# Token-order GLU, a three-engine rope and new buffer homes in a hybrid decoder block

## The chip, the cores and the metric

The kernel runs on the eight cores of one Trainium2 chip, one launch, one sequence of 2,048 tokens to a core. The time of a run is the device time of the slowest core, in microseconds (us). Each kernel was run several times, in alternation with the kernel before on the same chip, and all comparisons use such runs.

There is a second, slower state, whatever the kernel: in some executions the cores of one die, or of both, run at a lower granted TensorE clock and the whole takes longer. Runs in that state are left out below; "fast" means the others. A ratio is always the mean time of one kernel's fast runs over the mean of the other's in the same rounds, with a 95% interval, so it is not quite the ratio of the medians that stand beside it.

Names: PE is the matmul engine (TensorE), DVE is VectorE, ACT is ScalarE, Pool is GpSimd, SP is SyncE, which here only issues transfers. SBUF is a core's working memory, PSUM the buffer that matmuls write to, HBM the large memory of the chip; "granted clock" is the share of the full TensorE clock that the profile shows as allowed. Pool issues transfers too, on the software DMA queue; SP uses the hardware queue.

## The reference, cut to what matters

```python
D_MODEL, SEQ, D_FF = 2048, 2048, 5632
# per layer
xn = rms_norm(x, g_pre_mix)
q, k, v, u = split(xn @ w_in)                    # 1024, 256, 256, 1024 columns
q, k = rotary(q), rotary(k)                      # "rope"
attn = sliding_window_attention(q, k, v, sinks)  # window 128, blocks of 128 tokens
y = s5_ssm(u, ...)                               # diagonal complex scan, 64 groups of 16 channels
z = gelu(y)
ssm = z * sigmoid(z @ w_glu + b_glu)             # the GLU, 1024 channels
mix = concat(rms_norm(attn), rms_norm(ssm)) @ w_o
h = x + rms_norm(mix, g_post_mix)
out = h + rms_norm(swiglu(rms_norm(h)), g_post_ffn)   # feed-forward, 5632 wide
```

The result must agree with this within a tolerance.

## The kernel before

Instructions are first recorded, then put in one fixed order for each engine by a list scheduler inside the kernel. It uses priorities, dependences, and its own time estimate for each instruction. The lower its number `prio`, the earlier an instruction is placed. The estimates put nothing on the chip, but they decide the order, and on the chip each engine follows that order strictly.

The parts that the argument touches (cuts are marked `# ...`):

```python
# the scheduler's estimates
if eng == "vector":
    # ...
    return 0.065 + big / 960.0 / sp
# transfers: one pipe for all of them
b = max(dma_free, s + op.dur); dma_free = b + op.nb; op.fin = dma_free + 1.9

# rope: both products on DVE, straight from PSUM; the sum on Pool; ONE pair rA, rB
def rope(bk, tt, nh):
    n = nh * 64
    V.tensor_tensor(out=rA[:, 0:n], in0=ps[:, bk, 0:n], in1=cap(cosT, ...), op=ALU.mult)
    for t_ in range(2):
        V.tensor_tensor(out=rv[:, :, t_, :], in0=pv[:, :, 1 - t_, :], in1=cap(snT, ...), op=ALU.mult)
# in proj_q: qb = qr[tt % 2]; G.tensor_tensor(out=qb, in0=rA, in1=rB, op=ALU.add)
#            P.dma(qT[...], qb, transpose=True)

# GLU: z comes back from HBM by token residue j (token = 8 c + j)
wglu = sb(WSO, [128, 8, 1024], BF16)         # over the LAST projection's weights
def glu():
    P.dma(wglu[:, :, :], w_glu..., q="gpsimd")
    for tb in range(4):                      # 4 quarters of 512 tokens
        zt = zring[tb % 2]
        # ... two loads of z, four GELU of 1024 elements on ACT, SBUF to SBUF
        for e8 in range(8):
            mv = M1[:, e8, :].rearrange("p (c j) -> p j c", j=8)[:, 2*tb:2*tb+2, :]   # stride 8
            # 8 matmuls of 512 columns -> ps[bk]; tanh on ACT -> sg
            V.scalar_tensor_tensor(out=mv, in0=sg, scalar=1.0, in1=zt[:, e8, :], op0=ALU.add, op1=ALU.mult)
            G.tensor_tensor(out=sq, in0=mv, in1=mv, op=ALU.mult)
            T.matmul(ps[:, 7, :], lhsT=onesb, rhs=sq, ...)      # sum of squares over channels
        rstd(rbc, ps[:, 7, :], 1)
        for e8 in range(8):                  # the normalising multiply, in place
            V.scalar_tensor_tensor(out=mv, in0=mv, scalar=g_ssm[e8], in1=rbc, op0=ALU.mult, op1=ALU.mult)

# W_o in four quarters, 4 MB read and 2 MB written each
def load_wo(k):
    P.dma(Wo[k][:, :, :], w_o_v[:, 4*k:4*k+4, :], q="gpsimd")

# the order of recording and the priorities
# ... proj_u, ssm_pair 0..15, proj_q(0), proj_q(1)
P.prio = 300.0; load_w(0, 1024); proj_q(2)          # k and v, the last projection
# ... ssm_pair 16..31 at 90 + 6 q
P.prio = 400.0
attention(0); attention(1); glu()
for k in (3, 0, 1, 2): load_wo(k)
# then W_o projection of tile tt with attention of tile tt + 2; then feed-forward
```

The first two W_o quarters lie where the normalised input xnT lies, so they can load as soon as the last projection has read it. M1 holds the GLU's result, 8 x 2,048 bf16 per partition.

## Time and profile before

Median 2,960.0 us of 4 runs (2,955.1 to 2,963.3). The profiled run took 2,957.3 us on its slowest core.

| milestone, us from the start | before |
|---|---|
| the last input projection ends | 502.3 |
| first GLU matmul | 523.3 |
| last normalising multiply | 769.2 |
| first feed-forward matmul | 1,050.6 |
| end | 2,957.3 |

Below, "the GLU" is the stretch from the first GLU matmul to the last normalising multiply, and "the W_o stage" the stretch from there to the first feed-forward matmul.

The page's slices cut the span into 40 equal parts of 74 us. Each digit is a busy share in tenths; PEclk is the granted clock in tenths of full speed.

```profile
PE   3798997533698989999999999999999999999995
...
DVE  5828773477777731101101100002110010100003
...
PEclk9797898766899999999999999999999999999997
DMA  9775455600488879556556576669975565565545
```

From the sixteenth slice on, PE is full and nothing is to be had. The hole is in slices 8 to 11 (517 to 813 us): PE at 5, 3, 3 and 6 tenths, the clock at 7, 6, 6 and 8, and DVE at 4 and then 7.

The windows view gives the same in microseconds, for the stretches gap before the GLU, GLU, and W_o projection with attention. Columns: window, length, busy us of PE, PEld (weight loads), DVE, ACT and Pool with their instructions, granted clock, DMA share, GB/s.

```profile
502.00:523.00 21.00, 2.47 (x14) 1.11 (x14) 5.58 (x10) 5.28 (x6) 6.30 (x9) 0.63 0.89 144
523.00:769.00 246.00, 101.84 (x429) 41.83 (x436) 174.94 (x112) 68.40 (x87) 88.73 (x58) 0.68 0.23 54
769.00:1051.00 282.00, 246.21 (x1451) 116.30 (x1479) 194.18 (x323) 161.52 (x332) 105.42 (x115) 0.92 0.82 183
```

In the GLU's 246 us DVE works 175 and PE 102, at a clock of 0.68. Which DVE instructions these are, the groups view of that window shows (line, engine, operation, output<-inputs, shapes, count | busy us, mean ns | idle before); t_44 is M1:

```profile
L411 DVE SCALAR_TENSOR_TENSOR t_44<-t_44,t_54,t_53 128x512 bf16<-128x512 bf16 x32 | 75.0, 2660 | 21.6 <-ACT t_53 L411 21.6
L411 DVE SCALAR_TENSOR_TENSOR t_44<-t_144,t_142 128x512 bf16<-128x512 f32 x8 | 22.0, 2750 | 6.0 <-ACT t_144 L411 6.0
...
```

A multiply of 512 elements takes 2.66 us, a product of the group shown 2.75 (2.5 to 2.75 over all four groups). The chain of waits (start, length, what) confirms that runs of them end the stage, and shows what comes before it:

```profile
502.75 20.06 DMA t_143<-w_glu
...
600.89 23.26 DVE t_44 L411 x10
...
750.52 18.66 DVE t_44 L411 x8
```

The DMA view of the stretch around 500 us lists the issues with the time to landing; t_154 and t_155 are W_o quarters:

```profile
t_143<-w_glu POOLq DMA_DIRECT2D x1, 2048.0 KB, 20.1
t_154<-w_o POOLq DMA_DIRECT2D x1, 2048.0 KB, 30.7
t_155<-w_o POOLq DMA_DIRECT2D x1, 2048.0 KB, 39.9
```

In the same stretch SP's timeline (start, length, what) shows two attention transposes that took 10 and 23 us merely to be issued; ordinarily one takes 1.2:

```profile
508.31 9.67 SPq L411 DMA_TRANSPOSE t_150<-t_148  x1
518.02 22.97 SPq L411 DMA_TRANSPOSE t_151<-t_149  x1
```

PE did not feel this: it had the DVE-bound GLU to wait for anyway.

### The profile page before, as it was taken

How to read it: one execution, taken by the hardware profiler on the slowest of the kernel's cores; microseconds unless marked ns; L12 is line 12 of the kernel's file. 1: busy time of each engine (PE TensorE's matmuls, PEld its weight loads, DVE VectorE, ACT ScalarE, POOL GpSimd, SP SyncE). 2: the span in 40 equal slices, each digit the busy share in tenths (PEclk: the TensorE clock that was granted, in tenths of full speed). 3: DMA queues.
4: the chain of work that ended last, by engine and by line, in shares of the span. 5: the costliest groups of instructions: out<-in, count | busy, mean ns of one | idle time of the engine just before them, and what ended most of it. 6: DMA issues, size and time to landing. Idle time of an engine off the chain costs nothing.

```text
span 2957.3 us, 31078 instructions; the slowest of 8 cores (2936.6 to 2957.3 us)
## 1 busy us (share of the span) xinstructions
PE 2605.0 (88%) x12527; PEld 1199.9 (41%) x12768; DVE 909.2 (31%) x1293; ACT 627.3 (21%) x1217; POOL 559.5 (19%) x510
## 2 busy tenths in 40 slices
PE   3798997533698989999999999999999999999995
PEld 2444443211344434444444444444444444444442
DVE  5828773477777731101101100002110010100003
ACT  4534322421355641000000000012000000000002
POOL 4621332244343410000000111100000000011102
PEclk9797898766899999999999999999999999999997
DMA  9775455600488879556556576669975565565545
GB/s 199 197 155 121 82 111 109 120 22 15 114 192 194 192 161 127 71 72 86 72 72 86 72 131 102 101 91 245 199 114 74 70 84 76 71 103 79 75 71 211
DMA packets 489133, 335.38 MB, mean 113 GB/s; under 512 B 173216, under 2 KB 458272, under 8 KB 480288
## 3 DMA queue, kind: packets, MB, share of 16 engines
q0 software_dynamic: 252032, 159.46, 40.3%
q1 hardware_dynamic: 236960, 173.91, 22.3%
q8 instruction: 104, 1.70, 0.2%
q14 instruction: 37, 0.30, 0.0%
HBM read 398.26 MB, written 56.62 MB: 154 GB/s over the span
## 4 chain that ended last, share of the span: by engine, by line
PE 79%; DVE 8%; DMA 6%; ACT 2%; issue 2%; POOL 1%; SPq 1%; ACTq 0%; DVEq 0%; POOLq 0%
PE ps L411 79%; DVE t_44 L411 4%; DMA t_168<-w_up 2%; SPq L411 1%; DMA t_158<-x 1%; DMA t_143<-w_glu 1%; POOL t_146 L411 1%; DVE t_75 L411 1%; DMA t_167<-w_gate 1%; DMA t_188<-hscr 1%; DMA t_46<-t_113 1%; DVE t_76 L411 1%; ACT t_148 L411 0%; POOL t_147 L411 0%; DVE t_158 L411 0%
## 5 line engine op out<-in xcount | busy, mean ns | idle before, releaser
L411 PE MATMUL ps<-t_163,t_168 128*128 128x512 bf16 x1380 | 313.3, 382 | 18.3 <-DMA t_168<-w_up 16.9
L411 PE MATMUL ps<-t_163,t_167 128*128 128x512 bf16 x1380 | 310.9, 380 | 8.8 <-DMA t_167<-w_gate 7.4
L411 PE MATMUL ps<-t_163,t_166 128*128 128x512 bf16 x1377 | 308.6, 379 | 3.7 <-ACT ps L411 2.0
L411 PE MATMUL ps<-t_163,t_169 128*128 128x512 bf16 x1381 | 309.3, 379 | 1.4
L411 PEld LDWEIGHTS ps<-t_163,t_168 128*128 128x128 bf16 x1408 | 138.7, 99 | 185.6 <-issue 22.7
L411 PEld LDWEIGHTS ps<-t_163,t_167 128*128 128x128 bf16 x1408 | 138.2, 98 | 174.6 <-issue 9.8
L411 PEld LDWEIGHTS ps<-t_163,t_166 128*128 128x128 bf16 x1408 | 137.4, 98 | 168.4 <-issue 2.5
L411 PEld LDWEIGHTS ps<-t_163,t_169 128*128 128x128 bf16 x1408 | 137.6, 98 | 166.3
L411 DVE TENSOR_TENSOR t_183<-t_179,ps 128x512 bf16<-128x512 f32 x44 | 30.3, 688 | 427.4 <-PE ps L411 424.4
L411 ACT ACTIVATE ps<-ps 128x512 f32<-128x512 f32 x64 | 37.2, 582 | 574.8 <-DVE t_185 L411 286.5
L411 DVE TENSOR_TENSOR t_183<-t_181,ps 128x512 bf16<-128x512 f32 x44 | 30.3, 688 | 398.7 <-PE ps L411 398.7
L411 PE MATMUL ps<-t_48,t_43 128*128 128x512 bf16 x499 | 116.4, 390 | 8.0 <-DVE t_112 L411 6.6
L411 ACT ACTIVATE t_179<-ps 128x512 f32<-128x512 f32 x44 | 26.3, 597 | 421.5 <-PE ps L411 404.3
L411 ACT ACTIVATE t_181<-ps 128x512 f32<-128x512 f32 x44 | 26.3, 597 | 409.3 <-PE ps L411 409.3
L411 DVE TENSOR_TENSOR t_185<-ps,t_178 128x512 f32<-128x512 f32 x32 | 22.1, 690 | 277.4 <-PE ps L411 277.3
L411 POOL DMA_DIRECT2D t_167<-w_gate x22 | 25.2, 1144 | 423.3 <-PE ps L411 423.3
L411 POOL DMA_DIRECT2D t_166<-w_gate x22 | 25.3, 1148 | 392.8 <-PE ps L411 392.8
L411 DVE TENSOR_TENSOR t_179<-ps,t_178 128x512 f32<-128x512 f32 x8 | 5.5, 692 | 262.9 <-PE ps L411 255.6
L411 PE MATMUL ps<-t_156,t_44 128*128 128x512 bf16 x242 | 66.2, 395 | 20.2 <-DVE t_152 L411 18.3
L411 DVE SCALAR_TENSOR_TENSOR t_44<-t_44,t_54,t_53 128x512 bf16<-128x512 bf16 x32 | 75.0, 2660 | 21.6 <-ACT t_53 L411 21.6
L411 PE MATMUL ps<-t_174,t_183 128*128 128x512 bf16 x346 | 79.6, 379 | 0.9 <-DMA t_174<-w_down 0.6
L411 PE MATMUL ps<-t_172,t_183 128*128 128x512 bf16 x348 | 79.8, 379 | 0.2
(333 smaller groups left out, 3742.8 us busy)
## 6 DMA issues: line engine op xcount, KB each, us to landing
t_166<-w_gate POOLq DMA_DIRECT2D x22, 1024.0 KB, 9.1
t_168<-w_up POOLq DMA_DIRECT2D x22, 1024.0 KB, 10.8
t_167<-w_gate POOLq DMA_DIRECT2D x22, 1024.0 KB, 9.3
t_169<-w_up POOLq DMA_DIRECT2D x22, 1024.0 KB, 10.8
t_158<-x SPq DMA_DIRECT2D x16, 1024.0 KB, 6.4
hscr<-t_158 SPq DMA_DIRECT2D x16, 1024.0 KB, 5.3
t_184<-hscr SPq DMA_DIRECT2D x8, 1024.0 KB, 14.1
t_184<-ffscr SPq DMA_DIRECT2D x8, 1024.0 KB, 15.0
```

The lines of the kernel that those rows point to most:

```text
L411: inst = getattr(eng, m)(*a, **kw)
```

## The change

Its intent: take the strided writes out of the GLU. Each block of 128 channels of z is read back as it lies, 64 identity matmuls bring it into PSUM, and one GELU per 1,024 elements writes it to SBUF in token order. The GLU's products and multiplies are then contiguous. Half of its squares move from Pool to ACT. The rope's PSUM read moves to ACT, one product stays on DVE, the other goes to Pool, with work buffers doubled. SSM's rounding step moves from DVE to Pool. The input tiles, the SSM preparation, w_glu, one W_o quarter and the GLU buffers get other homes; an SSM work buffer called CL is doubled, and the buffer of SSM's scan result goes from two to one. In attention, two normalising multiplies become one instruction. The scheduler gets new time estimates (DVE 0.085 us more per instruction, Pool more per element, two DMA pipes that slow each other) and may use a second activation table set.

The core of the diff (buffer naming, homes and table sets are cut):

```diff
-            return 0.065 + big / 960.0 / sp
+            return 0.15 + big / 960.0 / sp
 ...
-                b = max(dma_free, s + op.dur)
-                dma_free = b + op.nb
-                op.fin = dma_free + 1.9
+                if e == "sync":
+                    b = max(hw_free, s + op.dur)
+                    if sw_free > b:
+                        hw_free = b + 1.6 * op.nb
+                        sw_free += op.nb
 ...
         def rope(bk, tt, nh):
+            rr, rA, rB, _ = rbuf[tt % 2 + (2 if nh == 4 else 0)]
-            V.tensor_tensor(out=rA[:, 0:n], in0=ps[:, bk, 0:n], in1=cap(cosT, ...), op=ALU.mult)
+            A.activation(out=rr[:, 0:n], in_=ps[:, bk, 0:n], func=AF.Copy)
+            V.tensor_tensor(out=rA[:, 0:n], in0=rr[:, 0:n], in1=cap(cosT, ...), op=ALU.mult)
             for t_ in range(2):
-                V.tensor_tensor(out=rv[:, :, t_, :], in0=pv[:, :, 1 - t_, :], ...)
+                G.tensor_tensor(out=rv[:, :, t_, :], in0=pv[:, :, 1 - t_, :], ...)
 ...
-            V.tensor_scalar(out=k[:, :], in0=y[:, :], scalar1=MAGIC, scalar2=MAGIC, ...)   # SSM rounding
+            G.tensor_scalar(out=k[:, :], in0=y[:, :], scalar1=MAGIC, scalar2=MAGIC, ...)
 ...
-        wglu = sb(WSO, [128, 8, 1024], BF16)
+        wglu = sb("wglu", WSO + 16 * KB, [128, 8, 1024], BF16)
+        def zconv():
+            for b in range(8):
+                zr = zraw[b % 2]
+                P.dma(zr[:, :, :], zscr[:, b * 128:(b + 1) * 128, :].rearrange("j p c -> p j c"), ...)
+                for h in range(2):
+                    bk = 4 + 2 * h
+                    for k in range(4):
+                        T.matmul(ps[:, bk + k // 2, ...], lhsT=identb[:, :],
+                                 rhs=zr[:, 2 * k:2 * k + 2, h * 128:(h + 1) * 128], start=True, stop=True)
+                    A.activation(out=zT[h][:, b, :].rearrange("p (c j) -> p c j", j=8),
+                                 in_=ps[:, bk:bk + 2, :].rearrange("p a (j c) -> p c (a j)", c=128), func=AF.Gelu_apprx_tanh)
 ...
-                    mv = M1[:, e8, :].rearrange("p (c j) -> p j c", j=8)[:, 2 * tb:2 * tb + 2, :]
-                    V.scalar_tensor_tensor(out=mv, in0=sg..., scalar=1.0, in1=zt[:, e8, :]..., ...)
-                    G.tensor_tensor(out=sq..., in0=mv, in1=mv, op=ALU.mult)
+                    V.scalar_tensor_tensor(out=M1[:, e8, ts_], in0=sg[:, :], scalar=1.0, in1=zt[:, e8, zs], ...)
+                    if e8 % 2 == 0:
+                        G.tensor_tensor(out=sq[:, :], in0=M1[:, e8, ts_], in1=M1[:, e8, ts_], op=ALU.mult)
+                    else:
+                        A.activation(out=sq[:, :], in_=M1[:, e8, ts_], func=AF.Square)
 ...
-        Wo = [sb(o_, ...) for o_ in (0, 16 * KB, WSO + 16 * KB, SO + 16 * KB)]
+        Wo = [sb("Wo", o_, ...) for o_ in (0, 16 * KB, WSO, SO + 16 * KB)]
 ...
         P.prio = 400.0
+        zconv()
         attention(0)
         attention(1)
         glu()
```

With w_glu moved, three W_o quarters, and no longer two, become loadable when the last projection ends: the third lies over that projection's weights.

## The prediction

> **What bounds it now.** The page's 40 slices show PE 95% busy from about 1,100 us to the end (feed-forward blocks, not changed). The loss lies before. Busy time by stretch: in 600 to 800 us PE is 45% busy, DVE 77%, granted clock about 0.7; in 150 to 475 us PE is 93% busy; in 820 to 1,050 us (W_o projection with attention) about 90%.
>
> The timeline dates the GLU: first matmul at 523 us, last normalising multiply at 769 us, so 246 us. PE's work there is 288 matmuls of 512 columns, at the 0.219 us of the feed-forward stage 63 us. The limit is DVE: 32 products of 2.5 to 2.75 us and 32 multiplies of 2.66 us (groups, 161 us together), because M1 is written with stride 8 elements. Four runs of multiplies stand in the chain of waits with 84 us. The Trainium skill, "SBUF — State Buffer", section "Door 1: The DMA port swizzle", says SBUF has 16-byte lines and that going to a new line each time pays a penalty; stride 8 bf16 is 16 bytes. The trace agrees: a contiguous 128x2048 instruction of this kind takes 2.37 us, about 0.6 us per 512 elements. Before the GLU, PE waits 14 us for w_glu, issued at 502.8 us because it lies in the last projection's weight buffer.
>
> **The change, costed.**
> - z to token order: 64 short identity matmuls (about 8 us PE); GELU keeps 16 instructions of 1,024 elements (1.05 us now; from PSUM with stride I assume 1.1 to 1.5), partly behind the k/v projection: 5 to 10 us exposed.
> - GLU: DVE 64 x about 0.65 = 42 us instead of 161; half the squares go to ACT. PE-bound: 9 x 0.219 = 2.0 us per step, 16 per quarter, plus 1 to 2 us for table loads (1.28 us each): 70 to 80 us. Saves about 165 us.
> - w_glu in the other weight buffer, free earlier: saves 14 to 20 us.
> - W_o: three quarters load after the k/v projection (43 us for three loads in the trace), one after half the GLU (it lies under z): ready about when the GLU ends.
> - Rope: DVE 1.5 us per tile falls to 0.7; ACT +0.6, Pool +1.5. PSUM frees sooner, so PE in 250 to 325 us (20 of 25 us busy, clock 0.65) fills better. SSM buffers no longer lie under preparation buffers, and the doubled CL removes Pool's 48 us of waiting on its store, so SSM may start before 209 us. Saves 20 to 35 us.
> - W_o stage: PE-bound, about 17.5 us per tile (DVE 14.5): same length, about 293 us after the GLU.
>
> **Sum.** 165 + 17 + 27 - 10 = about 200 us, nearly all on the critical path. Predicted 2,760 us, 2,715 to 2,815. Faster by over 2%: 0.96; within 2%: 0.03; slower: 0.01.
>
> **What would show it.** GLU 70 to 90 us; M1 writes 0.6 to 0.7 us; granted clock there above 0.9 (the skill, "TensorE: Matmul & The Clock Gate", Part 1: an idle PE falls to half clock, consistent with 0.7 here); no wait for w_glu; first feed-forward matmul near 850 instead of 1,050 us; feed-forward unchanged, about 1,860 us after the last W_o matmul.
>
> **What would make it wrong.** Pool and DVE slowing each other in the rope (a square on Pool took 9.5 us beside DVE's strided multiplies, 1.1 alone); GELU's PSUM read at stride 512 bytes costing 2 us or more; the last W_o quarter landing late; identity matmuls in PE's fixed order waiting for z loads.

## The result and the profile after

The changed kernel takes 2,878.95 us, the median of 4 runs (2,862.1 to 2,889.1); before 2,960.0. The ratio of the fast runs is 0.9722, interval 0.9668 to 0.9775: faster, by 82 us by the medians, where 200 were forecast. The result is correct. Within the fast runs there is a small spread: in two of the four, die 0 had a granted clock of 0.948 and took 2,884 to 2,887 us, against 0.958 and 2,858 to 2,862 us on die 1. The profiled run is one without that, 2,860.5 us, so the traces differ by 97 us. On undisturbed dies alone, the slowest cores of the changed kernel have a median of 2,860 us here and of 2,865 in its repeat below, which is about 0.967 of the kernel before.

| milestone, us | before | after | forecast (worked out from the sums of the prediction) |
|---|---|---|---|
| the last input projection ends | 502.3 | 486.7 | 475 |
| first GLU matmul | 523.3 | 551.7 | 489 |
| last normalising multiply | 769.2 | 659.6 | 570 |
| first feed-forward matmul | 1,050.6 | 941.6 | 851 |
| end | 2,957.3 | 2,860.5 | 2,758 |

The forecast column subtracts 27 (rope and SSM) from the first row; starts the GLU after a gap of 21 - 17 + 10 = 14 us; gives the GLU 246 - 165 = 81 us; and leaves the rest as it was. Against it, the profiled run loses 12 us in the projections, 51 us in the gap, 27 us in the GLU, 1 us in the W_o stage and 12 us in the feed-forward part.

The slices of the page after, to be held against those before:

```profile
PE   3789998489888989999999999989999999999994
...
DVE  7635863176766310001110000012111000000003
...
PEclk9789998689998989999999999999999999999997
DMA  9685743637888875646566666589965564665545
```

The hole has shrunk from four slices to one, the eighth (501 to 572 us): PE at 4 tenths, DVE at 1, and the clock at 6. The windows of the same three stretches:

```profile
487.00:552.00 65.00, 15.82 (x75) 8.19 (x73) 2.06 (x4) 21.31 (x23) 5.10 (x8) 0.54 0.83 160
552.00:660.00 108.00, 92.51 (x464) 39.95 (x462) 75.03 (x112) 70.96 (x104) 40.16 (x43) 0.90 0.37 81
660.00:942.00 282.00, 243.81 (x1463) 115.29 (x1464) 194.29 (x298) 158.04 (x324) 119.07 (x117) 0.93 0.83 181
```

The GLU shrank from 246 to 108 us and PE is now its busiest engine. The W_o stage is unchanged at 282. But the gap before the GLU grew from 21 to 65 us, in which PE works 16 and the DMA engines are 83% busy. The M1 writes did what was asked of them; the first line is the normalising multiply, the second one of four groups of products:

```profile
L430 DVE SCALAR_TENSOR_TENSOR M1.2_44<-M1.2_44,sm.12_54,rbc.11_53 128x512 bf16<-128x512 bf16 x32 | 26.3, 890 | 2.8 <-ACT rbc.11_53 L430 2.8
...
L430 DVE SCALAR_TENSOR_TENSOR M1.2_44<-sgb.115_157,zT.112_154 128x512 bf16<-128x512 f32 x8 | 7.7, 958 | 3.9 <-ACT sgb.115_157 L430 3.9
...
```

What PE waits for between 480 and 662 us (waited for: us in total, times, longest):

```profile
PE ps L430 <- DMA zraw.109_151<-zscr: 27.7, 2, 27.0
PE ps L430 <- DMA zraw.110_152<-zscr: 17.4, 3, 14.0
PE ps L430 <- ACT sgb.114_156 L430: 5.3, 3, 2.4
```

Waits for two of the eight z loads cost 27 and 14 us, 41 together. Later ones are quick, as the chain of waits shows:

```profile
491.51 42.52 DMA zraw.110_152<-zscr
...
538.44 4.18 DMA zraw.109_151<-zscr
...
```

And this is their company; the DMA view of 480 to 560 us, size and time to landing:

```profile
Wo.124_166<-w_o POOLq DMA_DIRECT2D x1, 2048.0 KB, 17.8
Wo.125_167<-w_o POOLq DMA_DIRECT2D x1, 2048.0 KB, 29.2
Wo.126_168<-w_o POOLq DMA_DIRECT2D x1, 2048.0 KB, 42.5
zraw.109_151<-zscr SPq DMA_DIRECT2D x3, 512.0 KB, 15.2
zraw.110_152<-zscr SPq DMA_DIRECT2D x3, 512.0 KB, 3.8
```

Pool issues three W_o quarters between 487 and 490 us, in the same moment in which SP issues the first z loads:

```profile
487.62 0.38 SPq L430 DMA_DIRECT2D zraw.109_151<-zscr  x1
...
491.51 7.76 SPq L430 DMA_DIRECT2D zraw.110_152<-zscr  x1
520.32 7.25 SPq L430 DMA_DIRECT2D zraw.109_151<-zscr  x1
536.16 0.36 SPq L430 DMA_DIRECT2D zraw.110_152<-zscr  x1
```

The first of these lands at 518 us, the second at 534, with the last W_o quarter, and the third, issued at 520, at 535. The three issued after that take about 4 us each, as did the two before the burst. Not one of the conversion's matmuls ran under the k and v projection: the first stands at 486.6 us, and the projection ended at 486.7. It is the burst that had held up two attention transposes before the change, when it cost nothing.

### The profile page after: what moved, and what is told of

Read it like the earlier page. It is cut to its first block, busy times and chain, and to the rows that moved or that the text cites. A ratio compares the mean times of both kernels' runs of the same rounds, so it can differ in the third digit from the quotient of the medians.

```text
span 2860.5 us, 31526 instructions; the slowest of 8 cores (2832.4 to 2860.5 us)
## 1 busy us (share of the span) xinstructions
PE 2606.5 (91%) x12832; PEld 1199.6 (42%) x12832; DVE 792.9 (28%) x1133; ACT 662.9 (23%) x1286; POOL 631.1 (22%) x622
## 4 chain that ended last, share of the span: by engine, by line
PE 80%; DMA 7%; DVE 4%; issue 3%; ACT 2%; POOL 1%; SPq 1%; ACTq 0%; DVEq 0%; POOLq 0%
PE ps L430 80%; DMA wup.138_180<-w_up 2%; DMA zraw.110_152<-zscr 1%; SPq L430 1%; DMA wgt.137_179<-w_gate 1%; DMA PT.120_162<-Pb.118_160 1%; DMA hring.158_200<-hscr 1%; DVE xs.34_76 L430 1%; DVE M1.2_44 L430 1%; ACT L427 0%; DMA idf.27_69<-ident 0%; ACT Pb.118_160 L430 0%; DVE TT.63_105 L430 0%; DVE xs.33_75 L430 0%; DVE ast.23_65 L430 0%
## 5 line engine op out<-in xcount | busy, mean ns | idle before, releaser
L430 PE MATMUL ps<-hnT.133_175,wgt.137_179 128*128 128x512 bf16 x1408 | 313.0, 381 | 15.8 <-DMA wgt.137_179<-w_gate 15.8
L430 PE MATMUL ps<-hnT.133_175,wup.138_180 128*128 128x512 bf16 x1408 | 312.3, 380 | 8.3 <-DMA wup.138_180<-w_up 8.3
L430 PE MATMUL ps<-hnT.133_175,wgt.136_178 128*128 128x512 bf16 x1408 | 311.1, 379 | 2.4 <-DMA wgt.136_178<-w_gate 2.4
L430 PE MATMUL ps<-hnT.133_175,wup.139_181 128*128 128x512 bf16 x1408 | 310.9, 379 | 0.0
L430 PEld LDWEIGHTS ps<-hnT.133_175,wgt.137_179 128*128 128x128 bf16 x1408 | 138.0, 98 | 183.9 <-issue 19.3
L430 PEld LDWEIGHTS ps<-hnT.133_175,wup.138_180 128*128 128x128 bf16 x1408 | 138.0, 98 | 175.9 <-issue 11.1
L430 PEld LDWEIGHTS ps<-hnT.133_175,wgt.136_178 128*128 128x128 bf16 x1408 | 137.9, 98 | 168.6 <-issue 2.9
L430 PEld LDWEIGHTS ps<-hnT.133_175,wup.139_181 128*128 128x128 bf16 x1408 | 137.7, 98 | 166.2
L430 DVE TENSOR_TENSOR hid.153_195<-ev.149_191,ps 128x512 bf16<-128x512 f32 x44 | 30.2, 687 | 438.2 <-PE ps L430 435.4
L430 DVE TENSOR_TENSOR hid.153_195<-ev.151_193,ps 128x512 bf16<-128x512 f32 x44 | 30.2, 687 | 390.5 <-PE ps L430 390.5
L430 ACT ACTIVATE ev.149_191<-ps 128x512 f32<-128x512 f32 x44 | 26.3, 597 | 420.5 <-PE ps L430 406.5
L430 ACT ACTIVATE ev.151_193<-ps 128x512 f32<-128x512 f32 x44 | 26.3, 597 | 399.0 <-PE ps L430 397.5
L430 PE MATMUL ps<-ws.6_48,xnT.1_43 128*128 128x512 bf16 x512 | 117.5, 386 | 0.0
L430 POOL DMA_DIRECT2D wgt.137_179<-w_gate x22 | 25.1, 1141 | 413.1 <-PE ps L430 413.1
L430 POOL DMA_DIRECT2D wgt.136_178<-w_gate x22 | 25.3, 1148 | 393.4 <-PE ps L430 393.4
L430 PE MATMUL ps<-Wo.124_166,qT.3_45 128*128 128x512 bf16 x256 | 71.6, 405 | 21.4 <-DVE Ab.129_171 L430 18.6
L430 PE MATMUL ps<-wdn.144_186,hid.153_195 128*128 128x512 bf16 x352 | 80.0, 379 | 0.8 <-DMA wdn.144_186<-w_down 0.8
L430 PE MATMUL ps<-wdn.147_189,hid.153_195 128*128 128x512 bf16 x352 | 80.1, 379 | 0.0
L430 PE MATMUL ps<-wdn.140_182,hid.153_195 128*128 128x512 bf16 x352 | 80.1, 379 | 0.0
L430 PE MATMUL ps<-wdn.146_188,hid.153_195 128*128 128x512 bf16 x352 | 80.1, 379 | 0.0
```

Of the source, the lines that this page charges most:

```text
L430: inst = getattr(eng, m)(*a, **kw)
```

## The experiments

The first theory: the burst of W_o loads beside the z loads makes the stall, and the stall is most of the miss. The rivals: the time merely moves to another wait; or the miss lies in the GLU and W_o stage themselves. There were eighteen runs, one of them the changed kernel again, in six batches, each batch beside the kernel before on its own chip. Every edit also lets the scheduler reorder the instructions around it. Gains over the changed kernel are given from both its ratios, 0.9688 and 0.9722; the second contains the two runs in which die 0 had less clock. On undisturbed dies alone (median of their slowest cores) the ratio is about 0.967 for the changed kernel and 0.956, 0.958, 0.947, 0.955 and 0.936 for experiments 1, 11, 12, 13 and 15, so the lower end of each range is the safer one.

### 1. The z conversion earlier

```diff
+        P.prio = 290.0
         zconv()
+        P.prio = 400.0
```

The z of a block is complete well before the last projection ends; with a priority ahead of the k and v projection its loads come before the burst.

> The changed kernel with the z conversion given a better priority than the k/v projection, so that its matmuls stand among the projection's and its z loads are issued before the three W_o loads. Theory (z loads caught behind W_o loads): the first GLU matmul moves from 551.7 to about 490-500 us after the start, the loads of z land in 3 to 6 us each, W_o still arrives in time, the total falls by 45 to 60 us, to about 2,825 us (ratio to before about 0.955). Rival (the conversion is slow by itself: 512-byte pieces, two buffers, PE taken from the projection): the conversion takes as long, the projection ends later by about as much, and the total falls by less than 15 us.

Measured: 2,839 us, ratio 0.9569 [0.9548, 0.959]. The conversion lies at 449 to 484 us, wholly under the projection, and the first GLU matmul comes at 488. So the 65 us gap is gone, but only 35 to 45 us of it are gained (0.0119 to 0.0153 of 2,960, against the changed kernel's 0.9688 to 0.9722). The chain of waits shows who now stands beside the burst:

```profile
493.54 37.51 DMA PT.120_162<-Pb.118_160
```

An attention transpose takes 37.5 us, and PE waits 20 us for that buffer. The stall was real, but the GLU now takes 152 us in place of 108, so a good part of its worth turned into other waits.

### 2. The W_o loads held until z has landed

```diff
-            P.dma(Wo[k][:, :, :], w_o_v[...], q="gpsimd")
+            P.dma(Wo[k][:, :, :], w_o_v[...], q="gpsimd", rk=[("zl", b) for b in range(8)])
```

> The changed kernel with the W_o loads made to wait until the last z load has landed; nothing else moves. Theory (contention with W_o): after the k/v projection the remaining z loads take about 4 us each, the conversion ends near 510-515 us, the GLU starts there instead of at 551.7 us, and W_o, landing by about 560-570 us and its last quarter by about 590 us, is still ahead of the W_o projection: total 30 to 45 us less, about 2,840 us. Rival (the conversion is slow by itself): the GLU starts at 540 us or later and the total is the same or longer, because W_o now comes later.

Measured: 2,862 us, ratio 0.9646 [0.9617, 0.9675]. The z loads beside the conversion take 4.6 to 5.7 us each and the conversion 26 us in place of 61, which shows that the burst made them slow. The first GLU matmul comes at 526 us. But PE then waits 18.9 us for one attention transpose, and the first feed-forward matmul comes at 940.5 us, as with the stall.

### 3. The old kernel with contiguous writes alone

Wrong result: the kernel before, M1 written in phase order (relative error 0.71).

```diff
-  mv = M1[:, e8, :].rearrange("p (c j) -> p j c", j=8)[:, 2 * tb:2 * tb + 2, :]
+  mv = M1[:, e8, tb * 512:(tb + 1) * 512].rearrange("p (a c) -> p a c", a=2)
```

> The kernel before with the two GLU writes of M1 made contiguous (phase order, so the result is wrong on purpose); no conversion, no moved buffer, same rope. Theory (stride of 16 bytes is the cost of the GLU): the 128x512 writes fall from about 2.7 to about 0.7 us, the GLU from 246 to about 95-105 us, the total by 130 to 150 us, to about 2,820 us, which is below the changed kernel. Rival (the GLU is bound by something else, such as PE's clock or ACT's table loads): the writes get faster but the total falls by less than 80 us.

Measured: 2,900 us, ratio 0.9765 [0.9746, 0.9785], a gain of 70 us and not 130 to 150. The products fall to 0.80 us and the multiplies to 1.25; the GLU falls from 246 to 148 us, so 98 us are won there. The GLU starts 4 us later, and the W_o stage grows from 281 to 305 and gives back a quarter. The stride is the cause of the slow GLU, and what a stage wins is not what the kernel wins.

### 4. The old rope

```diff
-            A.activation(out=rr[:, 0:n], in_=ps[:, bk, 0:n], func=AF.Copy)
-            V.tensor_tensor(out=rA..., in0=rr[:, 0:n], ...)
+            V.tensor_tensor(out=rA..., in0=ps[:, bk, 0:n], ...)
             for t_ in range(2):
-                G.tensor_tensor(out=rv..., ...)
+                V.tensor_tensor(out=rv..., ...)
```

> The changed kernel with the rope back on DVE from PSUM (its buffers kept). If the rope split is what moved the end of the projections from 502 to 487 us, that end goes back to 500 us or later and the total rises by 10 to 25 us, to about 2,895 us. Rival (the gain before the GLU comes from the buffers' new homes, or Pool and DVE hinder each other so that the split is worth nothing): the end of the projections stays within 5 us of 487 us and the total within 8 us.

Measured: 2,908 us, ratio 0.9816 [0.9787, 0.9845]; the projections end at 527 us, 41 us later than in the changed kernel, and even 25 us later than in the kernel before, which has the same rope on DVE. Read alone, this says that the rope move is worth 30 us or more. It is read again under 14.

### 5. to 8. Four parts that might matter

Number 6 spreads W_o in 16 pieces over the GLU steps, on top of experiment 1:

```diff
-            P.dma(Wo[k][:, :, :], w_o_v[:, 4 * k:4 * k + 4, :], q="gpsimd")
+            at = {0: (0, 1, 3, 4), 1: (6, 7, 9, 10), 2: (12, 13, 15, 16), 3: (18, 20, 22, 24)}[k]
+            for c in range(4):
+                P.dma(Wo[k][:, c, :], w_o_v[:, 4 * k + c, :], q="gpsimd", rk=[("g", at[c])])
```

> The conversion early as in the first experiment, and W_o loaded in 16 pieces of a quarter of its 4 loads, each tied to a step of the GLU, so that the software queue never holds 12 MB at once. In the first experiment the conversion was hidden, but a transpose of attention issued at 493.5 us took 37.5 us to land, beside three W_o loads issued at 488 to 491 us, and the GLU lasted from 488 to 625 us. Theory (any load on the other queue waits out a burst of W_o): transposes land in 3 to 6 us throughout, the GLU ends at 580 to 595 us, total about 30 to 40 us below the first experiment: about 2,800 us (ratio 0.944 to 0.948). Rival (the transposes and the GLU are slow for another reason, for example PE's clock after the projections, or W_o simply needs that bandwidth): the GLU still ends after 610 us and the total is within 12 us of the first experiment, or W_o arrives late and PE waits for it by as much.

Missed. Only two of its runs were fast, 2,877 us, ratio 0.9696 [0.9663, 0.9729], and the profile fell in the slow state (read on a core of the undisturbed die). The pieces were issued in bunches, at 495 to 501, 516 to 524 and 545 to 562 us, and PE waited 31 us in three waits for attention transposes behind them. A wait tied to steps of work does not spread transfers when the work itself runs in spurts.

Number 7 has all squares on Pool, as before the change (`if e8 % 2` and the ACT branch taken out):

> The changed kernel with all squares of the GLU on Pool again instead of half on ACT. In the contiguous variant of the kernel before, the normalising multiplies took 1.25 us beside Pool's squares, 0.89 us in the changed kernel. Theory (DVE with two inputs in SBUF and Pool reading SBUF take turns): the multiplies' mean goes from 0.89 to about 1.2 us, the GLU (first matmul to last multiply, 108 us) gets 10 to 20 us longer, total 8 to 20 us more. Rival (ACT, with twelve table loads, is the GLU's limit): taking the squares off ACT shortens the GLU, total lower by 5 us or more.

Measured: ratio 0.9654 [0.9583, 0.9725], lowest 2,851 us. The multiplies rise from 0.89 to 1.11 us and the GLU from 108 to 118, as expected, but the W_o stage gives the 10 us back: the first feed-forward matmul comes at 943.6 us. The share of ACT in the squares bought nothing in the total. The means hide two cases: in the changed kernel 25 of the 32 multiplies took 0.74 to 0.75 us, and the 7 that lay for over 0.5 us beside a square on Pool took 1.1 to 1.6; in this run 15 took 0.74 to 0.76 us and 17 took 1.1 to 1.5, all beside squares or softmax masks on Pool.

Number 5 restores the old homes of the input tiles and the SSM preparation:

> The changed kernel with x, its gain and the normalised rows back under the query buffer, and the preparation buffers back under the SSM buffers (doubled CL kept). Theory of the prediction (the new homes let the SSM start earlier): the second u projection ends at 236 us or later, the first SSM matmul comes later than 200 us by 5 us or more, the total rises by 5 to 15 us. Rival from the trace (new homes only let SSM loads of weights into the SP queue early, where they hold up the preparation's small transfers; PE waits 12.5 us for Kst): the second u projection ends at 224 us as before the change, and the total is the same or up to 12 us less.

Measured: 2,867 us, ratio 0.9665 [0.9639, 0.9692]; SSM's first matmul at 209.8 in place of 200.6 us, the projections end at 485.9. The homes make SSM start 9 us earlier and are worth nothing at the end.

Number 8 is the changed kernel once more:

> The changed kernel itself once more, on the same chip as the other three, as the base for their differences. All theories: ratio to before 0.967 to 0.978 as on record; z loads that are issued after 487 us land in 27 to 43 us, the first GLU matmul at 545 to 560 us.

Measured: lowest 2,864.8 us, ratio 0.9688 [0.9627, 0.975]; the conversion at 482.3 to 544.5, first feed-forward matmul at 940.3 us. The stall repeats: 65.8 us from the projections' end to the first GLU matmul, against 65.0.

### 9. GLU before attention

On top of experiment 1, the GLU is recorded and ranked before the first two attention tiles, so that PE does not stand behind a late transpose.

```diff
         P.exp0 = True
+        glu()
+        P.prio = 405.0
         attention(0)
         attention(1)
-        glu()
+        P.prio = 400.0
```

> The conversion early as in the first experiment, and the GLU ahead of the first two attention tiles (recorded first, better priority), so that no instruction of PE in the GLU waits for a transpose while W_o is loading; W_o itself as in the changed kernel. Theory (a transfer on the critical path that shares the time of the W_o burst waits it out; none is left now): no wait of PE for PT above 3 us before the last GLU product, GLU from 488 to 570-580 us, first feed-forward matmul at 880 to 895 us instead of 918, total about 2,800 us, ratio 0.943 to 0.950. Rival (the time only moves: the attention tiles put off leave the W_o stage that much longer, because that stage is not limited by PE): the GLU ends early as above, but the feed-forward starts at 910 us or later and the ratio is 0.953 to 0.960, as in the first experiment.

Measured: ratio 0.9672 [0.9644, 0.97], lowest 2,854 us. The GLU ran at 497 to 604 us without a long wait, and the W_o stage, from the last multiply to the first feed-forward matmul, took 342 us in place of 282: attention must be done some time, and there it is in the way. The rival was right in kind; the ratio is worse than even it expected.

### 10. SSM's rounding back on DVE

```diff
-            G.tensor_scalar(out=k[:, :], in0=y[:, :], scalar1=MAGIC, ...)
+            V.tensor_scalar(out=k[:, :], in0=y[:, :], scalar1=MAGIC, ...)
```

> The changed kernel with the rounding step of the SSM tables back on DVE (32 instructions of 128x256). With the rope back on DVE the projections ended at 527 us, 25 us later than before the change, so something else of the change must cost time in that stretch. Theory (Pool is too loaded: tables on Pool come late for DVE): projections end at 475 us or earlier, total 5 to 15 us less. Rival (it is not this step): projections end within 5 us of 482 to 487 us, or later, total within 6 us or longer.

Measured: ratio 0.9689 [0.9661, 0.9718], the projections end at 487.7 us. The step is worth nothing here.

### 11. The old time estimates

The scheduler's estimates of the kernel before in the changed kernel (the first hunks of the diff undone). No instruction changes, only the order.

> The changed kernel with the time estimates by which it orders its instructions (cost of each instruction, two DMA queues) put back to those of before; the instructions are the same. Theory (the order is worth little): projections end and GLU start within 10 us of 482-487 and 548-552 us, total within 10 us. Rival (the new order is what costs or wins in the projections and in the W_o stage): projections' end or the time from last GLU product to the feed-forward's start moves by over 15 us.

Measured: 2,841 us, ratio 0.9595 [0.9576, 0.9614], against 0.9688 to 0.9722 of the changed kernel: 27 to 38 us (21 between the two profiled runs, neither of them disturbed). The z stall is all there (PE waits 28.5 and 15.3 us for z), the GLU starts at 552 us, and still the first feed-forward matmul comes at 924.5 us, 16 us earlier. PE's wait for DVE's output tile in the W_o stage falls from 18.6 to 2.3 us. The new estimates were made with care and gave a worse order.

### 12. Both helpers together

Experiments 1 and 11 in one kernel.

> The changed kernel with both edits that helped alone: the z conversion placed ahead of the k and v projection (which measured a ratio of 0.957 to the kernel before) and the scheduler's time estimates of the kernel before (0.960; the changed kernel alone 0.969 to 0.972). Theory: they act on different stretches, so their gains add. With the old estimates the z conversion is hidden in the k/v projection as well: first GLU matmul at about 488 us instead of 552, and the W_o stage after it keeps the short waits of DVE's output (about 2 us in place of 18 us), so the first feed-forward matmul comes at about 895 to 908 us, the time is 2800 to 2825 us and the ratio about 0.945 to 0.952. Rival: what the one gains the stage after it takes back, because the attention transposes wait behind the three W_o loads wherever the z loads do not, and because the order of the later stages comes out differently anyway: the first feed-forward matmul stays at about 915 to 925 us and the ratio at 0.955 or above.

Measured: 2,808 us, ratio 0.948 [0.946, 0.9499], correct, as the theory had it: the gains add. It beats both kernels. First GLU matmul 486, last multiply 627, first feed-forward matmul 893 us. The burst still shows, in SP's timeline:

```profile
491.73 8.39 SPq L417 DMA_TRANSPOSE PT.120_162<-Pb.118_160  x1
500.17 28.89 SPq L417 DMA_TRANSPOSE PT.121_163<-Pb.119_161  x1
540.14 1.96 SPq L417 DMA_TRANSPOSE PT.120_162<-Pb.118_160  x1
```

No attention transpose is issued between 500 and 540 us; attention's first tiles fall behind the GLU.

### 13. and 15. Without the burst

Moving the loads or the conversion only turned one wait into another, so no run had shown the time without the burst. Here the three early W_o quarters load a sixteenth of their columns, and the matmuls repeat it (wrong result, relative error 0.93; the same number of matmuls). Once in the changed kernel, once in the kernel of experiment 12.

```diff
+            n = 2048 if k == 3 else 128
-            P.dma(Wo[k][:, :, :], w_o_v[:, 4 * k:4 * k + 4, :], q="gpsimd")
+            P.dma(Wo[k][:, :, 0:n], w_o_v[:, 4 * k:4 * k + 4, 0:n], q="gpsimd")
 ...
+            if c < 12:      # 128 columns, read four times
+                rhs = cap(Wo[c // 4], (c % 4) * 2048, [[8192, 128], [0, 4], [1, 128]])
```

Two of the three small loads then go out well before the projections end (at 424.9 and 426.5 us in experiment 13), so they are not only smaller.

> The changed kernel with the three early W_o loads cut to a sixteenth each (128 of 2048 columns, repeated by the matmuls; wrong result on purpose, same number of matmuls). It shows what the burst of loads costs in all. Theory: the burst is the main part of the miss. The z conversion then runs at the pace of its own loads, about 25 us as in the run where W_o waited for z, the attention transposes land in under 6 us, the first GLU matmul comes at about 512 us, the first feed-forward matmul at about 895 to 910, and the ratio is 0.950 to 0.957 (the changed kernel alone 0.969 to 0.972). Rival: the time only moves into the in-order waits of the W_o stage, as it did in three runs before: the first feed-forward matmul stays at 925 us or later and the ratio at 0.962 or above.

Measured: 2,828 us, ratio 0.9554 [0.9533, 0.9576]. The conversion takes 25 us; the GLU starts at 524 us (the projections ended at 496 in this order), and the first feed-forward matmul comes at 912. The ratio is in the theory's range; that last mark is 2 us outside it. In the changed kernel the burst costs 40 to 50 us, all told (36 on undisturbed dies). And even without it the gap before the GLU is 28 us where the forecast had 14.

> The best version so far (z conversion ahead of the k/v projection, old estimates; measured ratio 0.948) with the three early W_o loads cut to a sixteenth (wrong result on purpose). Theory: what the burst still costs there is the waits for attention transposes, 16 us in PE's list of waits, and the order of work behind them; without the burst the first feed-forward matmul comes at about 865 to 880 us instead of 893, the time is 2775 to 2795 us and the ratio 0.937 to 0.943. Rival: these waits are off the limiting path, the W_o stage has its own limit, and the ratio stays at 0.945 to 0.950.

Measured: 2,768 to 2,789 us, ratio 0.9361 [0.9334, 0.9388]; the first feed-forward matmul at 849.6 us, where the prediction had it "near 850". By the ratios that is 35 us better than experiment 12, a little more than the theory expected. (The profiled run is the slowest of the four, 2,789 us, only 16 us better than that of experiment 12.) SP's timeline, in which the same transposes now go out one after another:

```profile
489.33 1.23 SPq L417 DMA_TRANSPOSE PT.120_162<-Pb.118_160  x1
492.69 1.23 SPq L417 DMA_TRANSPOSE PT.121_163<-Pb.119_161  x1
495.74 1.23 SPq L417 DMA_TRANSPOSE PT.120_162<-Pb.118_160  x1
```

In this kernel the GLU stage takes 106 us and the W_o stage 259, against 140 and 267 in experiment 12. PE's waits for transposes there came to only 16 us, so the list of waits understated the burst by half; the rest may be the order of work behind it, which was not tested.

### 14., 16. and 17. What the rope is worth

Experiment 4 had left a contradiction: the old rope made the changed kernel slower than its like in the kernel before. The first run here is experiment 4 with the old estimates.

> The changed kernel with the old rope (on DVE from PSUM) and the old time estimates in the scheduler. Theory: the old rope ended the projections at 527 us and not at 502 because the new estimates (DVE 0.09 us more per instruction) put the instructions in an order that suits the new rope alone: with the old estimates they end at about 500 to 508 us, the z stall stays at about 64 us, the first feed-forward matmul comes at about 945 to 955, ratio 0.967 to 0.973. Rival: the estimates are not the reason (the single R buffer, the z store's home, or the z conversion's effect on the order are): they end at 518 us or later, ratio about 0.977 to 0.982.

Measured: 2,833 us, ratio 0.9571 [0.9549, 0.9592], and the projections end at 477.7 us, earlier than either theory had it. This is no slower than the new rope with the same estimates (experiment 11: 0.9595 [0.9576, 0.9614], 486.6 us). So with these estimates the rope's move to three engines brings nothing; what experiment 4 measured was the new estimates, which suit the old rope badly (0.9816 against 0.9571). And with the old rope the projections now end 25 us earlier than in the kernel before. Of the differences left, two were tried: the rounding step and the doubled work buffers. Back to DVE with the rounding, on top of 14:

> e14 (old rope on DVE, old estimates) with SSM's rounding step back on DVE as well, as in the kernel before. Theory: what shortens the stretch is relief of DVE, and with the rope on DVE the rounding step, 32 instructions, is the relief that e14 still has; without it the stall of the kernel before comes back: granted clock about 0.7 in 250 to 325 us, the projections end at 492 to 505 us, ratio 0.962 to 0.969 (e14 0.957). Rival: the step is worth nothing here either: 476 to 484 us and 0.955 to 0.959.

Measured: 2,835 us, ratio 0.9548 [0.9499, 0.9597], the projections end at 481.0 us. Not the rounding. Single work buffers, on top of 14:

```diff
-            rr, rA, rB, _ = rbuf[tt % 2 + (2 if nh == 4 else 0)]
+            rr, rA, rB, _ = rbuf[2 if nh == 4 else 0]
```

> e14 (old rope on DVE, old estimates) with single work buffers for the rope's two products, as in the kernel before. Theory of the buffers: with one pair, DVE must wait for Pool's sum of the last tile before it writes the next, so PSUM is held longer; the projections end at 490 to 505 us and the ratio is 0.962 to 0.969. Rival: DVE is busy with other work meanwhile, 476 to 484 us and 0.955 to 0.959.

Measured: 2,862 us, ratio 0.9639 [0.9592, 0.9686], and the projections end at 496.2 us, 18.5 later. So single buffers cost most of the 25 us, a gain that the prediction had put down to the rope's move. DVE's waits up to the projections' end show one way. First the kernel before, 225 to 502 us, where t_111 is the rope's first product and t_113 Pool's sum, which must have read the product of the tile before; then experiment 14; then experiment 17:

```profile
DVE t_111 L411 <- POOL t_113 L411: 25.9, 7, 15.1
```

```profile
DVE rA.73_115 L417 <- POOL qr.75_117 L417: 2.7, 1, 2.7
```

```profile
DVE rA.69_111 L417 <- POOL qr.71_113 L417: 12.2, 7, 3.7
...
DVE rA.69_111 L417 <- POOL qr.75_117 L417: 4.6, 4, 1.4
```

The product of a tile could not be written before Pool had added up the tile before. But these waits are not the whole answer. In time they all lie at 323 us or later: of the 25.9 us of the kernel before, 18.6 fall after 480 us, and in experiment 17 the first is at 332. The low clock lies earlier, as the windows show; the kernel before first, then experiment 14, then two of experiment 17:

```profile
275.00:300.00 25.00, 20.08 (x95) 8.74 (x95) 17.52 (x40) 7.97 (x23) 4.62 (x6) 0.64 0.32 88
```

```profile
275.00:300.00 25.00, 25.00 (x149) 12.14 (x148) 23.70 (x50) 12.12 (x32) 13.45 (x13) 1.00 0.44 107
```

```profile
275.00:300.00 25.00, 23.13 (x120) 10.45 (x118) 19.00 (x41) 10.70 (x29) 12.34 (x13) 0.80 0.37 93
300.00:325.00 25.00, 19.07 (x99) 8.58 (x96) 21.43 (x43) 13.27 (x35) 9.90 (x12) 0.68 0.42 106
```

DVE is busier in experiment 14, with the rope still on it, and PE is full at full clock, so DVE was not overloaded. With single buffers and nothing else edited, the low clock is back. Between 250 and 325 us PE ran about 50 matmuls of the projections in the kernel before, 121 in experiment 17 and 211 in experiment 14, beside 230 to 240 of SSM in each: with one pair, fewer projection matmuls stand there to fill PE. Whether the scheduler moved them because of the buffers, or PE met waits, was not separated.

### 18. W_o behind the first transposes

On top of 12: the first W_o load waits for tile 0's four transposes, the other three quarters for tile 1's.

```diff
-  P.dma(pt_[:, :, :], pb_..., transpose=True)
+  P.dma(pt_[:, :, :], pb_..., transpose=True, wk=[("pt", tt, j)])
 ...
-  P.dma(Wo[k][:, :, :], w_o_v[...], q="gpsimd")
+  P.dma(Wo[k][:, :, :], w_o_v[...], q="gpsimd", rk=[("pt", 0 if k == 0 else 1, j) for j in range(4)])
```

> e12 (z conversion ahead of the k/v projection, old estimates; 0.948) with the first W_o load held until the four attention transposes of tile 0 have landed and the others until those of tile 1 have: correct result. Theory: the transposes of both tiles then land in 3 to 6 us each, the loads still end before the W_o stage needs them or a few us late, and most of the gain of the run without the burst (0.936) stays: first feed-forward matmul at 855 to 875 us, ratio 0.938 to 0.944. Rival: the loads are too late, PE waits for W_o at the start of its stage or the later transposes take the wait: first feed-forward matmul at 885 us or later, ratio 0.946 or above.

Missed: ratio 0.9616 [0.958, 0.9652], lowest 2,849 us, worse than experiment 12. The order came out differently from the start (projections end at 502 us). The first four transposes went out in 1.2 us each, the sixth took 10.6; the last three W_o loads were issued at 564 to 566 us, a later transpose took 22 us to issue behind them, PE waited 37 us for ACT's softmax tiles, and the first feed-forward matmul came at 960 us. No correct kernel here has got the 35 us that experiment 15 shows.

### The main ratios at a glance

| kernel | ratio to before | first GLU matmul | first feed-forward matmul |
|---|---|---|---|
| changed | 0.9722; again 0.9688 | 552; 548 | 942; 940 |
| 1 z conversion early | 0.9569 | 488 | 918 |
| 2 W_o after z | 0.9646 | 526 | 941 |
| 9 GLU first | 0.9672 | 497 | 946 |
| 11 old estimates | 0.9595 | 552 | 925 |
| 12 = 1 + 11 | 0.9480 | 486 | 893 |
| 13 changed, no burst (wrong result) | 0.9554 | 524 | 912 |
| 15 = 12, no burst (wrong result) | 0.9361 | 485 | 850 |
| 18 = 12, W_o behind transposes | 0.9616 | 503 | 960 |

## Why the prediction was wrong

The direction and the main mechanism were right. The size was wrong by 119 us of the medians (100 us against the profiled run). Point by point:

**The strided writes: right.** The prediction took the 16-byte line of SBUF from the Trainium skill, "SBUF — State Buffer", section "Door 1: The DMA port swizzle": an access that goes to a new 16-byte line each time pays a penalty. The trace agrees: 2.66 us before and 0.89 after for the multiply, and experiment 3 shows the same with nothing else edited (products at 0.80). The home of w_glu was right as well: it is issued at 411.7 us, and PE has no wait for it.

**"partly behind the k/v projection: 5 to 10 us exposed": the step that failed.** The conversion was not exposed by 5 to 10 us; the gap before the GLU grew to 65 us where the forecast had 14. That is 51 us, half of the miss. It has two parts. The overlap was wrong: with a priority behind the projection's, none of the conversion ran under it, and even without the burst the conversion took 25 to 26 us and the gap was 28 to 30 (experiments 13 and 2), about 15 more than forecast. The burst added the other 35 or so. The prediction named the danger, "identity matmuls in PE's fixed order waiting for z loads", but gave it no microseconds. In the same list it had three W_o quarters loading after the k/v projection ("43 us for three loads in the trace"), and put that down as a question of when W_o is ready, and no more. The two belong to one moment: 12 MB of reads on one queue and the z loads on the other. The trace of before already had the price, in two transposes that took 10 and 23 us to issue beside three loads of the same size. Experiments 2 and 13 show that the z loads are quick without the burst.

The Trainium skill's page "DMA: Bandwidth & Descriptors", section "Queues, rings and completion order", would have warned: each DMA engine goes round robin between the queues it has work for, a packet at a time. In the window of 480 to 560 us the software queue moved 6.29 MB in 1,584 packets and the hardware queue 4.46 MB in 9,648, so about 3,970 against 462 bytes each. Turns taken by packet then give the z loads the smaller share of the bytes. That fits the measured 42.5 us, but no run here changed the packet size, so it is not shown.

**The GLU, "70 to 80 us": the size was too small.** The stage took 108 us. PE is its busiest engine (92.5 us), so the label fits. The estimate counted the GLU's own matmuls at full clock; the trace has attention tiles' matmuls in between (about 11 us), a granted clock of 0.90, and 11 table loads of 1.28 us on ACT. Experiment 15 without any stall had 106 us, so the 27 us are not a sequel of the burst. How they divide was not tested.

**"W_o stage: PE-bound, about 17.5 us per tile (DVE 14.5): same length": right by number, doubtful by reason.** It kept its 282 us. But PE works only 244 of them, and the order alone moved its end by 16 us (experiment 11), and its length ranged from 259 us (experiment 15) to 305 (experiment 3); the 342 of experiment 9 hold two attention tiles more. It is limited by waits in a fixed order as much as by PE. Which wait would have to go is open.

**The rope, "PSUM frees sooner" and "Saves 20 to 35 us": about right in size, wrong in cause.** The projections ended 16 us earlier, and the low clock of 250 to 325 us is gone (0.67, 0.64, 0.67 before; 0.90, 0.96, 1.00 after). But with the old estimates the old rope gives the same with doubled work buffers (experiment 14) and loses most of it with single ones (17). The engines did not matter there, nor the rounding (16); in the changed kernel, neither the homes (5) nor the rounding (10) did.

**Not in the prediction at all: the scheduler's estimates.** They cost 27 to 38 us by the ratios, 21 by the profiled runs.

The pieces together: the changed kernel at 0.9688 to 0.9722, the z conversion moved (0.9569), the estimates undone as well (0.948), the burst taken away as well (0.9361). From first to last these are 97 to 107 us, which is the size of the miss, and that last kernel's 2,768 to 2,789 us lies in the forecast range of 2,715 to 2,815. So the forecast was the time of a kernel in which those three things do not happen. That the sum fits is partly luck: its GLU is 25 us longer than forecast and its W_o stage 23 us shorter.

Open: why the W_o stage's length depends on the order as it does; how the GLU's extra 27 us divide; and why the feed-forward part is 12 us longer in the profile after (another core, other transfers at its start). Other schedules for W_o that keep the transposes going and still land in time may exist; the two that were tried (6 and 18) lost. No run undid the doubled CL, w_glu's home, the second activation table set or the merged attention multiply alone. A second buffer for SSM's scan result, which the kernel before had, was not tried either: in the place at hand it overlapped the rope's sine table.

## What to carry to other kernels

When a change puts a small transfer that PE waits for at the moment when big loads become free to start, price it at what small transfers took beside those loads, not at what they take alone. Before dividing work over more engines, try a second work buffer alone: here it gave what the division had been credited with. And where a scheduler orders the instructions, undoing one part also reorders the rest, so check a single undo under a second order before believing it.

## What the Trainium skill lacked or had wrong

- "DMA: Bandwidth & Descriptors" states the round robin by packet but gives no cost of a small hardware-queue transfer beside large software-queue loads. Here a 512 KB load took 30.6 and 42.5 us beside three loads of 4 MB read each, and about 4 us after them; attention transposes, which otherwise land in about 3 us, took 28 to 45 beside such loads (the kernel before, experiments 1, 2 and 12). It also lacks that the issuing instruction itself is held: 7.8 us for a load and up to 28.9 us for a transpose on SP, which ordinarily take 0.4 and 1.2, so that everything behind it in SP's order waits too.
- "PSUM — Partial Sum Buffer", section "Specifications (TRN2)", says that any non-contiguous access slows matmuls significantly, and says nothing of ACT. ACT's GELU reading PSUM at a stride of 512 bytes took 1,024 ns for 1,024 elements, against 1,046 ns for the contiguous SBUF form of the kernel before: no penalty.
- "SBUF — State Buffer", section "Door 1: The DMA port swizzle", names the penalty for a new 16-byte line without a size. For a DVE instruction with two inputs and a write at 16-byte stride it was 2.66 us for 512 bf16 elements (in place, so the read is strided as well), against 0.89 contiguous, or 0.74 to 0.75 for the contiguous ones with no square on Pool beside them.
- The same page, section "Who interferes with whom", says that a DVE instruction with two SBUF inputs contends with a Pool instruction that reads SBUF. The runs agree and give sizes: the multiply took 0.74 to 0.75 us alone and 1.1 to 1.6 when it lay beside a square on Pool, a mean of 0.89 us with half the squares on Pool, 1.11 with all of them (experiment 7), 1.25 in experiment 3; the rope's product took 0.85 to 0.91 us from SBUF beside Pool, 0.68 from PSUM.
